# A 3x3 convolution with residual: x loaded as fp32 through the hardware queue of residual and output, and cast to bf16 while it is packed

## The chip, the core and the metric

The kernel runs on one core of a Trainium2 chip. The core has five engines that matter here: TensorE (PE) multiplies matrices, VectorE (DVE) and ScalarE (ACT) work element by element, GpSimd (POOL) and SyncE (SP) here mainly issue transfers. Sixteen DMA engines move data between the chip's memory (HBM) and the core's on-chip memory (SBUF, 128 partitions). A DMA that is issued by SP or ACT goes through a hardware queue; one that is issued by POOL goes through a software queue, and the cast of x during the transfer is written as such a DMA. The metric is the device time of one execution in microseconds, as a median over runs.

## The reference

A batch of 16 images with 64 channels of 64 x 64 pixels is convolved with a 3 x 3 kernel (64 channels in, 64 out, padding 1), and a residual is added. Inputs and output are fp32.

```python
x_pad = np.pad(x, ((0, 0), (0, 0), (pad, pad), (pad, pad)), mode='constant')
for b, co, ci, kh, kw in all_indices:
    output[b, co] += weight[co, ci, kh, kw] * x_pad[b, ci, kh:kh+h, kw:kw+w]
return (output + residual).astype(np.float32)
```

Read from HBM are x and residual, 16.78 MB each, and 0.15 MB of weights; written are 16.78 MB.

## The kernel before

**Tiling.** Two images make a pair: 2 x 64 channels fill the 128 partitions, 4096 pixels each. There are eight pairs. A pair of x is loaded into a tile `xr` (bf16, five buffers, L48), a pair of the residual into a tile `ro` (fp32, one tile for each of the eight pairs, L47). The result is added into `ro` in place and stored from there, so a DMA of a pair moves 2.097 MB on the HBM side.

**Loads.** `load_x` (L53, L54) is issued by POOL and casts fp32 to bf16 during the transfer. `load_ro` (L56, L57) is issued by SP. At the start the weights are loaded by ACT's queue (L102), x pairs 0 to 4 by POOL (L103 to L106) and all eight residual pairs by SP (L107, L108). The x pairs 5 to 7 are issued by POOL as buffers come free: in `pack`, after the second image of a pair has been packed (L67, L68).

**Packing.** `pack(n)` (L59 to L68) puts image n into a tile `xp` (four buffers) so that even rows lie in partitions 64 to 127 and odd rows, shifted by one, in partitions 0 to 63. DVE copies the even rows (L65), ACT the odd rows (L66), 64 x 2048 elements each, bf16 to bf16.

**Convolution.** `convolve(n)` (L70 to L86) does 6 x 4 matmuls of 128 x 128 by up to 512 columns: three horizontal shifts, two row offsets, four chunks of eight rows of pairs. The weights are in a tile `wl` with zero blocks, so that one matmul makes even and odd output rows together. The result fills one of two PSUM buffers.

**Add and store.** `add(n)` (L88 to L98) adds PSUM and residual on DVE with two instructions of 64 x 2048 elements (L94). After the second image of a pair SP stores the pair (L98).

**Weights.** They are loaded into `wdup` (64 x 576 fp32), doubled by DVE (L117), transposed by PE in nine small steps with an identity matrix that POOL makes (L121), and cast into `wl` by six DVE copies (L132).

**Order.** The schedule is written out by hand: each engine runs its instructions in the order in which the program names them. `pack(0)` and `pack(1)` come first; then, for n from 0 to 15, `convolve(n)`, `pack(n + 2)`, `add(n)`. SP's queue has the eight residual loads and behind them the eight stores; POOL's queue has the x loads.

Of the kernel before, what the change touches and what calls it, by code (L numbers as in the profile page):

```python
# [1 line left out]

# [5 lines left out]

FP32 = mybir.dt.float32
BF16 = mybir.dt.bfloat16  # L10
ADD = mybir.AluOpType.add


@with_exitstack
def kernel(
    ctx: ExitStack,
    tc: tile.TileContext,
    x: bass.AP,
    weight: bass.AP,
    residual: bass.AP,  # L20
    out: bass.AP,
):
    nc = tc.nc

    B, C, H, W = x.shape
    CO = weight.shape[0]
    K = weight.shape[2]
    assert C == 64 and CO == 64 and K == 3 and H == 64 and W == 64 and B == 16

    NPIX = H * W  # L30
    NPAIR = B // 2
    J = H // 2
    JC = 8
    NCHUNK = J // JC
    NXR = 5

    res_bc = residual.rearrange("b c h w -> (b c) (h w)")
    out_bc = out.rearrange("b c h w -> (b c) (h w)")
    x_bc = x.rearrange("b c h w -> (b c) (h w)")
    w_flat = weight.rearrange("co ci kh kw -> co (ci kh kw)")  # L40

    pool = ctx.enter_context(tc.tile_pool(name="pool", bufs=1))
    psum = ctx.enter_context(tc.tile_pool(name="psum", bufs=2, space=bass.MemoryType.PSUM))

    wdup = pool.tile([64, 2, 576], FP32)
    ident = pool.tile([64, 64], FP32)
    ro = [pool.tile([128, NPIX], FP32, name=f"ro{p}") for p in range(NPAIR)]  # L47
    xr = [pool.tile([128, NPIX], BF16, name=f"xr{i}") for i in range(NXR)]  # L48

    xp = [pool.tile([128, J + 1, W], BF16, name=f"xp{i}") for i in range(4)]  # L50
    wl = pool.tile([128, 2, 3, 2, 64], BF16)

    def load_x(p):  # L53
        nc.gpsimd.dma_start(out=xr[p % NXR][:, :], in_=x_bc[128 * p : 128 * p + 128, :])  # L54

    def load_ro(p):  # L56
        nc.sync.dma_start(out=ro[p][:, :], in_=res_bc[128 * p : 128 * p + 128, :])  # L57

    def pack(n):  # L59

        p, im = divmod(n, 2)
        hp = slice(64 * im, 64 * im + 64)
        x4 = xr[p % NXR].rearrange("q (j two w) -> q j two w", two=2, w=W)
        t = xp[n % 4]
        nc.vector.tensor_copy(out=t[64:128, 0:J, :], in_=x4[hp, :, 0, :])  # L65
        nc.scalar.copy(out=t[0:64, 1 : J + 1, :], in_=x4[hp, :, 1, :])  # L66
        if im == 1 and p + NXR < NPAIR:  # L67
            load_x(p + NXR)  # L68

    def convolve(n):  # L70
        t = xp[n % 4]
        ps = psum.tile([128, NCHUNK, JC, W], FP32, name="ps")
        order = [(1, 0), (1, 1), (0, 0), (0, 1), (2, 0), (2, 1)]
        for i, (kw, d) in enumerate(order):
            xlo, xhi = max(0, 1 - kw), min(W, W + 1 - kw)
            for c in range(NCHUNK):
                j0 = JC * c
                nc.tensor.matmul(  # L78
                    out=ps[:, c, :, xlo:xhi],
                    lhsT=wl[:, d, kw, :, :].rearrange("q r c -> q (r c)"),  # L80
                    rhs=t[:, j0 + d : j0 + d + JC, xlo + kw - 1 : xhi + kw - 1],
                    start=i == 0,
                    stop=i == len(order) - 1,
                    skip_group_check=True,
                )
        return ps  # L86

    def add(n, ps):  # L88
        p, im = divmod(n, 2)
        hp = slice(64 * im, 64 * im + 64)  # L90
        o4 = ro[p].rearrange("q (j two w) -> q j two w", two=2, w=W)
        psj = ps.rearrange("q c j w -> q (c j) w")
        for par in range(2):
            nc.vector.tensor_tensor(  # L94
                out=o4[hp, :, par, :], in0=psj[64 * par : 64 * par + 64, :, :], in1=o4[hp, :, par, :], op=ADD
            )
        if im == 1:
            nc.sync.dma_start(out=out_bc[128 * p : 128 * p + 128, :], in_=ro[p][:, :])  # L98


    with tc.manual_schedule():
        nc.scalar.dma_start(out=wdup[:, 0, :], in_=w_flat[:, :])  # L102
        load_x(0)  # L103
        make_identity(nc, ident[:, :])
        for p in range(1, NXR):
            load_x(p)  # L106
        for p in range(NPAIR):  # L107
            load_ro(p)  # L108

        for t in xp:  # L110
            nc.vector.memset(t[0:64, 0, :], 0.0)  # L111
            nc.vector.memset(t[64:128, J, :], 0.0)  # L112
        nc.vector.memset(wl[0:64, 0, :, 1, :], 0.0)  # L113
        nc.vector.memset(wl[64:128, 1, :, 0, :], 0.0)  # L114


        nc.vector.tensor_copy(out=wdup[:, 1, :], in_=wdup[:, 0, :])  # L117
        wdup3 = wdup.rearrange("p d (ci t) -> p (d ci) t", t=9)
        tp = psum.tile([128, NCHUNK, JC, W], FP32, name="ps")
        for t in range(9):  # L120
            nc.tensor.transpose(out=tp[:, t // 8, t % 8, :], in_=wdup3[:, :, t], identity=ident[:, :])  # L121
        tpf = tp.rearrange("p c j w -> p (c j) w")
        for half, d, par, kh in (
            (0, 0, 0, 0),
            (1, 0, 0, 1),
            (1, 0, 1, 0),
            (0, 1, 0, 2),
            (0, 1, 1, 1),
            (1, 1, 1, 2),
        ):  # L130
            hp = slice(64 * half, 64 * half + 64)
            nc.vector.tensor_copy(out=wl[hp, d, :, par, :], in_=tpf[hp, 3 * kh : 3 * kh + 3, :])  # L132

        pack(0)
        pack(1)
        for n in range(B):
            ps = convolve(n)
            if n + 2 < B:
                pack(n + 2)
            add(n, ps)  # L140


# [1 line left out]
_INS = ['x', 'weight', 'residual']  # L144
_OUTS = [((16, 64, 64, 64), 'float32')]


# [23 lines left out]
```

## Time and profile before

| what | value |
|---|---|
| median of 7 runs | 125.5 us (125.38 to 125.86) |
| the profiled execution | 125.64 us, of which the span from first to last instruction is 123.9 |
| PE, DVE, ACT, POOL busy | 89.3, 87.6, 31.6, 4.9 us |
| a pack copy on ACT, on DVE | 1.90 us, 0.69 us (64 x 2048, bf16) |
| an add on DVE | 2.29 us (64 x 2048, fp32) |
| matmuls of the convolution | 88.1 us in all, from 18.36 to 106.42 |
| weights, issue to landing | 10.1 us |
| x pair, residual pair, output pair: median from issue to landing | 42.4, 43.5, 31.3 us |
| granted TensorE clock, mean | 0.941 |

The profile shows one execution. Its page has the busy share of each engine in 40 equal slices of the span (a 9 is 90% or more), the share of the 16 DMA engines that were busy and the GB/s that landed, a table of DMA queues, and the chain of work that ended last. A table by windows gives, for a stretch of time, the busy time of PE, weight loads, DVE, ACT and POOL, then the granted clock, the DMA share and the GB/s. A DMA's time from issue to landing includes the time in which it waited behind others in its queue.

### The profile page before, as it was taken

The numbers are of one execution on the slowest core, as the hardware profiler recorded it, in microseconds if no ns is written. First come the engines' busy times: TensorE is split into PE (matmuls) and PEld (weight loads), VectorE is DVE, ScalarE is ACT, GpSimd is POOL, SyncE is SP. The second block draws the span as 40 slices with busy tenths as digits, with TensorE's granted clock in tenths as the row PEclk, the third lists the DMA queues.
The fourth block names the chain that finished last, engine by engine and source line by source line (L and its number), as shares of the span: only waits on it lengthen the run. The fifth ranks groups of instructions, "written<-read, shape, count | busy, mean of one in ns | idle before, by whom it ended". The sixth has DMA issues, their size and how long they took to land.

```text
span 123.9 us, 1002 instructions
## 1 busy us (share of the span) xinstructions
PE 89.3 (72%) x393; PEld 38.4 (31%) x393; DVE 87.6 (71%) x65; ACT 31.6 (26%) x17; POOL 4.9 (4%) x14
## 2 busy tenths in 40 slices
PE   0003109999999999999999999999999999300000
PEld 0003003344344444443434344444444444000000
DVE  3001640059999999999999999999999999780000
ACT  4000065056038009108307505603800000000000
POOL 6400001000100010000000000000000000000000
PEclk9999999999999999999999999999999999965555
DMA  5999999999999999999999999999999999999990
GB/s 111 359 326 302 357 312 296 328 339 299 312 341 299 325 339 307 307 344 331 302 341 336 296 336 320 296 320 421 434 423 418 450 429 434 439 429 429 423 386 16
DMA packets 3540, 42.15 MB, mean 340 GB/s; under 512 B 400, under 2 KB 400, under 8 KB 464
## 3 DMA queue, kind: packets, MB, share of 16 engines
q1 hardware_dynamic: 2304, 33.56, 64.8%
q0 software_dynamic: 1152, 8.39, 32.3%
q10 hardware_dynamic: 80, 0.15, 0.3%
q8 instruction: 3, 0.05, 0.1%
q14 instruction: 1, 0.01, 0.0%
HBM read 33.70 MB, written 16.78 MB: 408 GB/s over the span
## 4 chain that ended last, share of the span: by engine, by line
PE 71%; DMA 12%; DVEq 2%; DVE 2%; ACT 2%; issue 1%; POOLq 0%
PE ps L78 71%; DMA xr<-in_x_dram 12%; DVEq L166 2%; DVE ro L94 2%; ACT xp L66 2%; POOLq L155 0%; POOLq masks.py:199 0%
## 5 line engine op out<-in xcount | busy, mean ns | idle before, releaser
L78 PE MATMUL ps<-xp,wl 128*128 128x504 bf16 (+1 forms) x384 | 88.0, 388 | 5.7 <-ACT xp L66 5.7
L94 DVE TENSOR_TENSOR ro<-ps,ro 64x2048 f32<-64x2048 f32 x32 | 73.2, 2289 | 1.5 <-PE ps L78 0.9
L78 PEld LDWEIGHTS <-wl 128*128 128x128 bf16 x384 | 37.3, 99 | 56.1 <-issue 11.3
L66 ACT COPY xp<-xr 64x2048 bf16<-64x2048 bf16 x16 | 30.4, 1897 | 56.4 <-DMA xr<-in_x_dram 56.2
L65 DVE COPY xp<-xr 64x2048 bf16<-64x2048 bf16 x16 | 11.0, 689 | 10.5 <-DMA xr<-in_x_dram 10.1
L121 PE MATMUL ps<-ident,wdup 64*128 64x64 f32 x9 | 1.3, 319 | 11.4 <-DVE wdup L117 11.4
L117 DVE COPY wdup<-wdup 64x576 f32<-64x576 f32 x1 | 0.5, 452 | 8.7 <-DMA wdup<-in_weight_dram 8.7
L54 POOL DMA_DIRECT2D xr<-in_x_dram x8 | 4.4, 555 | 38.7 <-DVE xp L65 21.9
L121 PEld LDWEIGHTS ps<-ident,wdup 64*128 64x128 f32 x9 | 1.1, 206 | 11.4 <-issue 11.4
L132 DVE CAST wl<-ps 64x192 bf16<-64x192 f32 x6 | 2.0, 352 | 1.5 <-PE ps L121 1.4
L66 ACT ACT_TABLE_LOAD x1 | 1.3, 1283 | 1.3 <-PEq L155 1.3
L111 DVE MEMSET xp<- 64x32 uint32 x4 | 0.3, 85 | 0.9 <-PEq L155 0.8
L112 DVE MEMSET xp<- 64x32 uint32 x4 | 0.3, 85 | 0.2
masks.py:199 POOL TENSOR_SCALAR_AFFINE_SELECT ident<-ident 64x64 f32<-64x64 f32 x1 | 0.2, 228 | 0.1
L114 DVE MEMSET wl<- 64x96 uint32 x1 | 0.1, 138 | 0.1
L113 DVE MEMSET wl<- 64x96 uint32 x1 | 0.1, 138 | 0.1
masks.py:197 POOL MEMSET ident<- 64x64 f32 x1 | 0.2, 171 | 0.0
L155 POOL MEMSET const-float32-0.0<- 128x1 f32 x1 | 0.1, 104 | 0.2 <-issue 0.2
L155 POOL MEMSET const-bfloat16-1.0<- 128x1 bf16 x1 | 0.1, 107 | 0.0
L155 POOL MEMSET const-uint8-127<- 128x1 uint8 x1 | 0.1, 107 | 0.0
L155 POOL MEMSET const-float32-1.0<- 128x1 f32 x1 | 0.1, 103 | 0.0
## 6 DMA issues: line engine op xcount, KB each, us to landing
ro<-in_residual_dram SPq DMA_DIRECT2D x8, 2048.0 KB, 43.5
out_dram<-ro SPq DMA_DIRECT2D x8, 2048.0 KB, 31.3
xr<-in_x_dram POOLq DMA_DIRECT2D x8, 1024.0 KB, 42.4
wdup<-in_weight_dram ACTq DMA_DIRECT2D x1, 144.0 KB, 10.1
```

Source lines behind the costliest of these rows:

```text
L54: nc.gpsimd.dma_start(out=xr[p % NXR][:, :], in_=x_bc[128 * p : 128 * p + 128, :])
L65: nc.vector.tensor_copy(out=t[64:128, 0:J, :], in_=x4[hp, :, 0, :])
L66: nc.scalar.copy(out=t[0:64, 1 : J + 1, :], in_=x4[hp, :, 1, :])
L78: nc.tensor.matmul(out=ps[:, c, :, xlo:xhi], lhsT=wl[:, d, kw, :, :].rearrange("q r c -> q (r c)"), rhs=t[:, j0 + d : j0 + d + JC, xlo + k ...
L94: nc.vector.tensor_tensor(out=o4[hp, :, par, :], in0=psj[64 * par : 64 * par + 64, :, :], in1=o4[hp, :, par, :], op=ADD)
L111: nc.vector.memset(t[0:64, 0, :], 0.0)
L112: nc.vector.memset(t[64:128, J, :], 0.0)
L117: nc.vector.tensor_copy(out=wdup[:, 1, :], in_=wdup[:, 0, :])
L121: nc.tensor.transpose(out=tp[:, t // 8, t % 8, :], in_=wdup3[:, :, t], identity=ident[:, :])
L132: nc.vector.tensor_copy(out=wl[hp, d, :, par, :], in_=tpf[hp, 3 * kh : 3 * kh + 3, :])
L155: nc = _bacc.Bacc("TRN2", target_bir_lowering=False, num_devices=1)
L166: with _tile.TileContext(nc) as tc:
```

## The change

x is loaded as fp32 by SP, in turn with the residual: x0, residual 0, x1, residual 1, x2, residual 2 at the start, and then one further pair of each when n is even and a buffer is to come free. `xr` holds fp32 and has three buffers in place of five. The cast to bf16 is done by the copies of `pack`; both halves are now copied by ACT, except for images 0 and 1, where DVE still copies the even rows. The weights are loaded by POOL, and `wdup` has no tile of its own: it lies in the tile of residual pair 7, whose load comes late. Stores are issued apart from `add`: pairs 0 to 3 after images 9, 11, 13 and 15, which in SP's order is behind all loads, and pairs 4 to 7 at the end.

```diff
-    NXR = 5
+    NXR = 3
...
-    wdup = pool.tile([64, 2, 576], FP32)
...
-    xr = [pool.tile([128, NPIX], BF16, name=f"xr{i}") for i in range(NXR)]
+    xr = [pool.tile([128, NPIX], FP32, name=f"xr{i}") for i in range(NXR)]
...
+    wdup = ro[NPAIR - 1][0:64, 0:1152].rearrange("p (d f) -> p d f", d=2)
...
-        nc.gpsimd.dma_start(out=xr[p % NXR][:, :], in_=x_bc[128 * p : 128 * p + 128, :])
+        nc.sync.dma_start(out=xr[p % NXR][:, :], in_=x_bc[128 * p : 128 * p + 128, :])
...
-        nc.vector.tensor_copy(out=t[64:128, 0:J, :], in_=x4[hp, :, 0, :])
+        first = nc.vector.tensor_copy if n < 2 else nc.scalar.copy
+        first(out=t[64:128, 0:J, :], in_=x4[hp, :, 0, :])
         nc.scalar.copy(out=t[0:64, 1 : J + 1, :], in_=x4[hp, :, 1, :])
-        if im == 1 and p + NXR < NPAIR:
-            load_x(p + NXR)
...
-        if im == 1:
-            nc.sync.dma_start(out=out_bc[128 * p : 128 * p + 128, :], in_=ro[p][:, :])
+
+    def store(p):
+        nc.sync.dma_start(out=out_bc[128 * p : 128 * p + 128, :], in_=ro[p][:, :])
...
-        nc.scalar.dma_start(out=wdup[:, 0, :], in_=w_flat[:, :])
-        load_x(0)
+        nc.gpsimd.dma_start(out=wdup[:, 0, :], in_=w_flat[:, :])
         make_identity(nc, ident[:, :])
-        for p in range(1, NXR):
+        for p in range(NXR):
             load_x(p)
-        for p in range(NPAIR):
             load_ro(p)
...
             if n + 2 < B:
                 pack(n + 2)
+            p, im = divmod(n, 2)
+            if im == 0 and p + NXR < NPAIR:
+                load_x(p + NXR)
+                load_ro(p + NXR)
             add(n, ps)
+            if n >= 9 and n % 2 == 1:
+                store((n - 9) // 2)
+        for p in range((B - 9) // 2 + 1, NPAIR):
+            store(p)
```

## The prediction

> **What bounds the kernel now.** I read the page's slices first, then the table of DMA queues, then the windows by stage, then the chain of work that ended last.
>
> ```profile
> PE   0003109999999999999999999999999999300000
> ...
> DMA  5999999999999999999999999999999999999990
> GB/s 111 359 326 302 357 312 296 328 339 299 312 341 299 325 339 307 307 344 331 302 341 336 296 336 320 296 320 421 434 423 418 450 429 434 439 429 429 423 386 16
> ```
>
> The DMA engines are full from the second slice to the last but one. TensorE starts in the sixth slice and is done four slices before the end. So the transfers set the time, although PE is busy throughout the middle. The GB/s row counts bytes where they land, which is why it rises to about 430 after slice 27: from there only stores are left.
>
> ```profile
> q1 hardware_dynamic: 2304, 33.56, 64.8%
> q0 software_dynamic: 1152, 8.39, 32.3%
> ...
> HBM read 33.70 MB, written 16.78 MB: 408 GB/s over the span
> ```
>
> The columns are packets, MB landed and share of 16 engines' span. The shares sum to 97.5% with the small queues: 120.8 of 123.9 us. The rest, 3.1 us, is the start and the end.
>
> ```profile
> 0.56 0.06 issue
> 0.62 0.02 POOLq L155
> 0.64 0.59 issue
> 1.23 0.00 POOLq masks.py:199
> 1.23 15.16 DMA xr<-in_x_dram
> ...
> 18.36 88.06 PE ps L78 x384
> 106.42 0.02 issue
> 106.45 2.29 DVE ro L94
> 108.73 2.31 DVEq L166
> ```
>
> The chain (start, length, what) goes through PE, but that is misleading: it ends at 111.0, when the last store is issued. That store then waits for the transfers ahead of it and takes 11.5 us to land (the shortest of the eight), more than twice the 4.9 us that 2.097 MB take at 429 GB/s. So compute ends about 6 us before it would delay the last store: 11.5 less 4.9, less about 1 us for starting and finishing.
>
> **The bytes of the change.** HBM traffic does not change: x is read as fp32 in both kernels, 50.48 MB in all. What lands in SBUF grows by 8.39 MB, because x no longer shrinks on the way. Does that cost DMA time? The table of queues answers: q0 took 32.3% of 123.9 = 40.0 us for 16.78 MB read and 8.39 landed; q1 took 64.8% = 80.3 us for 33.56 MB, or 40.1 us per 16.78. A packet of x costs what its source bytes cost, so the cast in the DMA saves nothing and the extra landed bytes cost 0.1 us at most.
>
> [...]
>
> **The rate of the transfers.** What remains is how fast loads run on one queue instead of two in turn.
>
> ```profile
> 2.00:3.50 1.50, 0.00 (x0) 0.00 (x0) 0.14 (x1) 0.59 (x1) 1.43 (x5) 1.00 0.68 175
> 3.50:5.50 2.00, 0.00 (x0) 0.00 (x0) 0.00 (x0) 0.00 (x0) 0.95 (x2) 1.00 0.94 390
> 12.00:82.00 70.00, 64.33 (x282) 27.49 (x281) 58.33 (x40) 26.56 (x14) 1.59 (x3) 1.00 1.02 320
> 86.00:119.00 33.00, 20.41 (x93) 8.65 (x91) 23.94 (x12) 3.35 (x2) 0.00 (x0) 0.85 1.00 429
> ```
>
> The last two columns are DMA share and GB/s landed. In 12 to 82 x and residual share the engines; both are read through at about 85 us, so equally. Of two packets one lands half its bytes, so the source rate is 320 x 4/3 = 427 GB/s. In 86 to 119 one hardware queue works alone (stores) at 429. The trace's packet records say the same with more digits: a 16 KB packet takes 624 ns when the queues alternate, 611 when one queue works alone, loads at the start among them; counted per engine, one such packet goes every 612 ns in the mixed stage and every 608 in the stores. Before 5.5 us only the residual's queue moves bulk data, so the rows at 2.0 and 3.5 are loads on one hardware queue: 0.68 of the engines at first, then 0.94 and 390 GB/s.
>
> The loads are 2 x 16.78 = 33.55 MB. At 427 they take 78.6 us. At 429 they take 78.2, a gain of 0.4; by the packet counts (128 packets per engine, 4.4 ns each) 0.56. I take **0.5 us**. The bounds: at 390 GB/s (the 3.5 to 5.5 row, still warming up) 86.0 us, a loss of 7.4; and at the 451 that the two half-microsecond windows from 4.5 to 5.5 average (463 and 439), 74.4 us, a gain of 4.2. I choose the store row because it is a steady stage of one hardware queue, while the other two are short and belong to the start; the packets of 611 ns among the first loads speak for it.
>
> The start is unchanged: SP issues its first DMA at 0.75 us in both, now x instead of residual. The weights are 0.15 MB in both.
>
> [...]
>
> **The edits that cost nothing, and their cover.** All lie beside full DMA engines.
>
> - Weights go from ACT's queue to POOL's, ahead of the identity. Their landing took 10.1 us with three queues; POOL's issue is at 1.23. From landing to the last cast of wl the trace has 10.89 to 14.76 = 3.9 us. With bounds of 6 and 15 us for the landing, wl is ready between 11 and 20; I take 14.
> - x0 goes first, alone on its queue: the first residual landed 10.8 us after its issue, sharing; x0 should land by 9 to 11.
> - The DVE halves of images 0 and 1 now read fp32: between 0.69 (the bf16 copy) and 2.29 us (the fp32 add of the same shape) each. Convolution 0 then starts near 15 (12 to 23) instead of 18.4.
> - From image 2 on ACT does both halves. The bf16 copy is 1.90 us; for fp32 input I take the same, bounds 0.69 and 2.29. So 3.8 us (at most 4.6) per image, under PE's 88.1/16 = 5.5. DVE loses 0.69 per image and keeps 2 x 2.29 = 4.6.
> - Supply: a pair x, residual takes 2 x 4.9 = 9.8 us, and PE uses a pair in 11.0. So PE does not starve: done at 15 + 88.1 = 103, last add at 108 (105 to 116).
> - SP's order: the load of x(p+3) waits for ACT's last pack of pair p. When x(p) lands, five DMAs (24 us) are still queued; packing takes 4 x 1.9 = 7.6 us, a few more where the tile xp is not yet free. So over 10 us of work is always queued, and residual(p+3), behind the waiting load on SP, is not late. The four early stores are issued only after all loads, with their adds long done; they too find the queue full.
> - The ninth hardware DMA already waits for the first ("SPq L57 <- DMA wdup" 6.3 us). If each DMA waits for the eighth before it, seven are still queued: no hole.
> - The last store's turn comes at 120.4 - 4.9 = 115.5 us. Its add is done near 108: 7 us of cover. Once convolution 0 starts after 23, each us counts in full.
>
> **The sum.** The profiled run took 125.64 us: span 123.9 and 1.7 around it. 125.64 - 0.5 = 125.14. The median of the runs, 125.5, lies 0.14 lower, so in terms of a median I say **125.0**.
>
> **Rivals.**
>
> 1. *Loads alone on one queue leave gaps*, which the software queue's packets fill today. For it: the 0.68 and 0.94 shares before 5.5 us, and the mixed stage's share of 1.02 against 1.00, so packets overlap more with two queues. Against it: stores on one queue run at 429, and the first loads' packets settle at 611 ns. It decides from a load rate below 425 GB/s (78.9 us, 0.25 more than now). Midway between 390 and 427, at 408, loads take 82.2 and the time is 129.1; 420 gives 126.8. Chance 0.18.
> 2. *Nothing changes*: a load packet has its slot of 612 ns whichever queue it is in, because HBM reads set it. The trace cannot part reads from the alternation after 12 us. Time 125.5. Chance 0.20.
> 3. *Compute ends late*: weights behind a full queue start convolution 0 at 25 instead of 15; the last add is then at 118, 2.2 us behind the last store's turn: 127.7. The 7 us of cover speak against it. Chance 0.04.
> 4. *A larger gain*: loads near 440 (76.3 us), or the engines finishing closer together at the end; now the last slices show 386 and 16 GB/s, so some stop before others. Time 123 to 124.2. Chance 0.08.
>
> The forecast itself, 124.2 to 125.25, has 0.50.
>
> **Numbers.** About 0.2% (0.25 us) is what a measurement of this kernel can tell from no change. Faster by more: forecast and rival 4, 0.58. Within: rival 2, 0.20. Slower: rivals 1 and 3, 0.22. The range leaves out most of rival 4 (0.07) and the part of rivals 1 and 3 above 126.8 (0.13): 124.2 to 126.8.
>
> **What would show it.** In the changed profile: one bulk queue with about 97% of the engines' time and 50.3 MB; GB/s near 429 from the third slice on, level over loads and stores; no DMA slice under 9 between; convolution 0 near 15 us and the last add near 108, with several us before the last transfer; a span near 123.4. A load stage of 415 or less, with a share below 1.0, would be rival 1; a DMA slice of 7 or 8 in the middle would mean that SP was late; a last store that starts moving as soon as it is issued, rival 3.

## The result, and the profile after

The changed kernel takes **125.95 us** (median of 25 runs, 125.55 to 126.47) against 125.44 for the kernel before (62 runs, 125.08 to 125.86). The ratio is 1.0038, with a 95% interval from 1.0030 to 1.0046: slower by about 0.5 us, where 0.5 us faster was forecast. The profiled execution took 126.02 us with a span of 124.2.

The page of the changed kernel, its slices (TensorE, DMA share, GB/s landed):

```profile
PE   0004499999999999999999999999999800000000
...
DMA  5999999999999999999999999999999999999990
GB/s 106 383 339 427 427 427 427 422 427 427 422 438 433 433 427 422 427 427 427 427 422 417 433 433 422 433 438 427 427 427 422 427 438 438 427 443 427 433 401 37
```

The DMA engines are as full as before, with no hole in the middle, and GB/s is level over loads and stores. One slice stands out: the third, 339 GB/s, with the engines marked full. The convolution starts one slice earlier (14.2 us against 18.4) and ends earlier.

The table of queues (packets, MB, share of 16 engines):

```profile
q1 hardware_dynamic: 3456, 50.33, 96.2%
q0 software_dynamic: 48, 0.15, 0.4%
q8 instruction: 3, 0.05, 0.2%
```

All bulk data is on one queue. A line of before is missing, "q14 instruction: 1": it will matter.

The end of the chain of waits (start, length, what):

```profile
14.21 84.84 PE ps L78 x384
99.04 0.02 issue
99.06 2.28 DVE ro L94
101.35 2.31 DVEq L173
```

Compute is done at 103.7 us and the last store then takes 19 us to land: compute is further from the bound than before. The copies that moved are no cost in themselves:

```profile
L67 ACT CAST xp<-xr 64x2048 bf16<-64x2048 f32 x14 | 26.5, 1896 | 20.2 <-DMA xr<-in_x_dram 20.0
L68 ACT CAST xp<-xr 64x2048 bf16<-64x2048 f32 x16 | 30.4, 1898 | 8.0 <-DMA xr<-in_x_dram 7.7
...
L67 DVE CAST xp<-xr 64x2048 bf16<-64x2048 f32 x2 | 2.4, 1220 | 0.0
```

An fp32 copy on ACT takes 1.90 us like the bf16 one, and ACT's idle time waits for x.

The windows by stage answer the question of the rate (DMA share and GB/s are the last two columns):

```profile
3.50:5.50 2.00, 0.00 (x0) 0.00 (x0) 0.00 (x0) 0.00 (x0) 0.00 (x0) 1.00 0.95 401
12.00:82.00 70.00, 67.80 (x306) 30.34 (x307) 57.35 (x29) 49.52 (x27) 0.00 (x0) 1.00 1.01 428
86.00:119.00 33.00, 13.03 (x61) 5.68 (x58) 15.83 (x7) 1.15 (x1) 0.00 (x0) 0.76 1.01 431
```

The loads run at 428 GB/s landed; before they landed 320, which is 427 at the source. Counted in packets of 16 KB at the source, 1826 go by in these 70 us, against 1825 before: in both one every 612 ns per engine, when the time of instruction fetches is left out. The loads alone on one queue gained nothing; the gap to the stores (431, every 608 to 609 ns) stayed.

So where do the 0.5 us come from? Two places, at the two ends. First the window from 6 to 12 us, before:

```profile
6.00:12.00 6.00, 0.56 (x5) 0.59 (x6) 0.45 (x1) 0.00 (x0) 0.00 (x0) 1.00 1.05 315
```

and after:

```profile
6.00:12.00 6.00, 1.26 (x9) 1.11 (x9) 1.44 (x4) 2.29 (x2) 0.00 (x0) 1.00 1.01 377
```

The 315 hold x at half its source bytes; the 377 do not. Counted in packets of 16 KB read or stored, 150 went by before and 130 after. In the packet records of the changed kernel bulk packets stretch from 611 to as much as 1026 ns between 5.8 and 8.4 us; the weights' packets alternate with them from 5.7 to 7.7. Before, the weights had alternated (4.9 to 9.3 us) with packets of 624 ns, of which after 5.5 us none took more than 696.

Second, the very end, in SP's own waits (total, times, longest). Before:

```profile
SPq L166 <- PEq L166: 0.6, 2, 0.5
```

After:

```profile
SPq L173 <- PEq L173: 0.9, 2, 0.8
```

These are the two meetings after the last store has landed, where the engines wait for one another. The longer one grew by 0.3 us. The last instructions show who is late. In the trace PE, ACT, DVE and SP each end with a drain, which raises the semaphore that the meeting waits for. VectorE's last drain starts at 123.39 us and takes 19 ns before; after, it starts at 123.90, 0.4 us behind the drains of the other engines, and takes 124 ns.

The two profiled executions add up like this: the last landing is 0.50 us later (122.56 to 123.05); SP then passes through its remaining semaphores in 0.09 us where it had needed 0.51, so 0.42 are won back; the meetings take 1.10 us where they had taken 0.79, 0.31 lost. Together 0.39; the spans differ by 0.37.

### The profile page after: what moved, and what is told of

Same layout as the page of the kernel before. It is cut to its first block, busy times and chain, and to the rows that moved or that the text cites. A ratio compares the mean times of both kernels' runs of the same rounds, so it can differ in the third digit from the quotient of the medians.

```text
span 124.2 us, 994 instructions
## 1 busy us (share of the span) xinstructions
PE 86.1 (69%) x393; PEld 39.0 (31%) x393; DVE 79.0 (64%) x51; ACT 58.2 (47%) x31; POOL 1.3 (1%) x7
## 4 chain that ended last, share of the span: by engine, by line
PE 69%; DMA 6%; DVE 5%; DVEq 2%; issue 1%; POOLq 0%
PE ps L78 68%; DMA ro<-in_weight_dram 6%; DVEq L173 2%; DVE ro L94 2%; DVE wl L131 2%; PE ps L120 1%; DVE xp L67 1%; DVE ro L116 0%; POOLq L162 0%; POOLq masks.py:199 0%
## 5 line engine op out<-in xcount | busy, mean ns | idle before, releaser
L78 PE MATMUL ps<-xp,wl 128*128 128x504 bf16 (+1 forms) x384 | 84.8, 385 | 3.2 <-DVE xp L67 3.2
L78 PEld LDWEIGHTS <-wl 128*128 128x128 bf16 x384 | 37.9, 99 | 49.9 <-DVE xp L67 3.4
L67 ACT CAST xp<-xr 64x2048 bf16<-64x2048 f32 x14 | 26.5, 1896 | 20.2 <-DMA xr<-in_x_dram 20.0
L68 ACT CAST xp<-xr 64x2048 bf16<-64x2048 f32 x16 | 30.4, 1898 | 8.0 <-DMA xr<-in_x_dram 7.7
L120 PE MATMUL ps<-ident,ro 64*128 64x64 f32 x9 | 1.3, 320 | 9.7 <-DVE ro L116 9.7
L116 DVE COPY ro<-ro 64x576 f32<-64x576 f32 x1 | 0.5, 451 | 7.0 <-DMA ro<-in_weight_dram 7.0
L120 PEld LDWEIGHTS ps<-ident,ro 64*128 64x128 f32 x9 | 1.1, 205 | 9.7 <-issue 9.7
L67 DVE CAST xp<-xr 64x2048 bf16<-64x2048 f32 x2 | 2.4, 1220 | 0.0
L103 POOL DMA_DIRECT2D ro<-in_weight_dram x1 | 0.6, 647 | 0.8 <-POOLq L162 0.8
```

Of the source, the lines that this page charges most:

```text
L67: first(out=t[64:128, 0:J, :], in_=x4[hp, :, 0, :])
L78: nc.tensor.matmul(out=ps[:, c, :, xlo:xhi], lhsT=wl[:, d, kw, :, :].rearrange("q r c -> q (r c)"), rhs=t[:, j0 + d : j0 + d + JC, xlo + k ...
L103: nc.gpsimd.dma_start(out=wdup[:, 0, :], in_=w_flat[:, :])
```

## The experiments

Time is the median in us; "ratio" is against the kernel before as measured beside it, with its 95% interval. "By 12 us" counts bulk packets of 16 KB at the source that have gone by 12 us; "mean end" is when the 16 engines had finished the last store, on average, and "last" the slowest of them; "meeting" is the longest wait in the SP line above. The last four come from one profiled execution of each.

| kernel | time | ratio | by 12 us | mean end | last | meeting |
|---|---|---|---|---|---|---|
| before | 125.44 | | 227 | 120.85 | 122.17 | 0.5 |
| changed | 125.95 | 1.0038 (1.0030 to 1.0046) | 209 | 121.53 | 122.72 | 0.8 |
| weights on ACT | 125.97 | 1.0050 (1.0035 to 1.0065) | 216 | 121.30 | 122.70 | 0.8 |
| before, weights on POOL | 125.57 | 1.0017 (1.0004 to 1.0029) | 208 | 121.60 | 122.58 | 0.5 |
| weights twice | 127.14 | 1.0142 (1.0116 to 1.0168) | 185 | 122.44 | 124.13 | 0.8 |
| weights in own tile | 126.02 | 1.0052 (1.0033 to 1.0071) | 212 | 121.43 | 122.95 | 0.8 |
| weights first on SP | 125.83 | 1.0033 (1.0021 to 1.0044) | 219 | 121.01 | 122.35 | 0.8 |
| that, and a load into 64 partitions | 127.14 | 1.0135 (1.0121 to 1.0149) | 197 | 121.99 | 123.47 | 0.8 |
| that, and a load into 128 partitions | 126.26 | 1.0067 (1.0050 to 1.0084) | 211 | 121.35 | 122.76 | 0.8 |
| x on ACT's hardware queue | 125.85 | 1.0033 (1.0021 to 1.0045) | 221 | 121.07 | 122.40 | 0.8 |
| before, weights first on SP | 125.55 | 1.0015 (1.0004 to 1.0025) | 226 | 120.97 | 122.14 | 0.5 |
| cast in the DMA again | 125.97 | 1.0041 (1.0026 to 1.0056) | 209 | 121.56 | 122.61 | 0.8 |
| fp32 through the software queue | 125.87 | 1.0040 (1.0025 to 1.0054) | 214 | 121.32 | 122.56 | 0.8 |
| more instructions on VectorE | 125.72 | 1.0025 (1.0013 to 1.0037) | 209 | 121.61 | 122.96 | 0.5 |
| that, and weights first on SP | 125.55 | 1.0015 (1.0006 to 1.0023) | 218 | 121.11 | 122.39 | 0.4 |

The column "by 12 us" gives "mean end" to within 0.2 us in all rows: a packet less is 611/16 = 38 ns, so the 18 packets between before and changed are 0.69 us, and the mean ends differ by 0.68. From 12 to 82 us all fifteen move between 1823 and 1829 packets, with whatever queue and type x has. So after the start the bulk transfers differ by 0.2 us at most.

### The weights at the start

The first theory was that the weights on the software queue are the loss. Four kernels: the weights back on ACT; the kernel before with the weights on POOL; the weights loaded twice; the weights in a tile of their own.

```diff
-        nc.gpsimd.dma_start(out=wdup[:, 0, :], in_=w_flat[:, :])
+        nc.scalar.dma_start(out=wdup[:, 0, :], in_=w_flat[:, :])
```

> The changed kernel, with the weights issued by ACT's hardware queue as before, nothing else undone. Theory A (the weights' transfer through the software queue slows the bulk packets beside it: in the changed profile 129.8 bulk packets' worth of 16 KB moved between 6 and 12 us, against 150.2 before, a loss of 20 packets x 611 ns / 16 engines = 0.8 us): the window 6 to 12 goes from 377 GB/s to about 405 and the time falls by 0.5 to 0.8, to 125.2 to 125.5, level with the kernel before. Theory B (the loss belongs to x running on the single hardware queue at the start, whatever the weights do): the window stays near 377 and the time near 125.95. Theory C (nothing at the start; the loads on one queue are slower throughout): 125.95 as well, with the window 12 to 82 below that of before.

Measured: 125.97. The window from 6 to 12 us rose only part of the way:

```profile
6.00:12.00 6.00, 1.27 (x9) 1.11 (x9) 0.89 (x3) 2.07 (x2) 0.00 (x0) 1.00 1.01 395
```

Bulk packets beside ACT's weights still took up to 791 ns. The mean end came 0.23 us earlier, the slowest engine did not. Theory A as worded (the software queue) falls; so does C's premise for the rate (428 in the load stage). The window is above B's 377, though the time is as B and C had it.

```diff
-        nc.scalar.dma_start(out=wdup[:, 0, :], in_=w_flat[:, :])
+        nc.gpsimd.dma_start(out=wdup[:, 0, :], in_=w_flat[:, :])
```

> The kernel before, with only the weights moved to POOL's software queue, ahead of x pair 0. Theory A: slower than before by 0.5 to 0.8, to 125.9 to 126.2, with hardware packets of the residual stretched beyond 700 ns while the weights move. Theories B and C: within 0.2 of 125.44.

Measured: 125.57, ratio 1.0017, that is 0.2 us slower (0.05 to 0.36). The stretch is there as theory A said (packets of up to 1036 ns, 208 by 12 us), but the time moved by much less than the 0.5 to 0.8 that it asked for. The mean end is 0.75 us later; the slowest engine only 0.41, and SP's last semaphores take 0.08 us instead of 0.51, because the last store is now among the last that it looks at.

```diff
         nc.gpsimd.dma_start(out=wdup[:, 0, :], in_=w_flat[:, :])
+        nc.gpsimd.dma_start(out=wdup[:, 1, :], in_=w_flat[:, :])
...
-        nc.vector.tensor_copy(out=wdup[:, 1, :], in_=wdup[:, 0, :])
```

> The changed kernel, with the weights loaded twice by POOL (the second load in place of VectorE's copy that doubles them), so twice the suspected cost. Theory A: the slow stretch is about twice as long and the time rises by 0.5 to 1.2 over 125.95, to 126.4 to 127.1, of which 0.4 would be the packets themselves. Theories B and C: at most 0.4 more, the engines' time of 0.15 MB more.

Measured: 127.14, 1.2 us more, just above what A expected. Of these, 0.4 are an estimate of the added packets' own time, from the 0.3% of the engines' span that the weights took before; by 12 us 24 packets fewer than in the changed kernel have gone by. So here the second load cost more than the 0.4 estimated for its own packets.

```diff
-    wdup = ro[NPAIR - 1][0:64, 0:1152].rearrange("p (d f) -> p d f", d=2)
+    wdup = pool.tile([64, 2, 576], FP32)
```

> The changed kernel, with the weights in a tile of their own instead of in residual tile 7, still loaded by POOL. If the place in SBUF matters in theory A, the slow stretch shrinks and the time falls toward 125.4; if the queue matters, it stays at 125.95 within 0.2. Theories B and C: 125.95.

Measured: 126.02, within the 0.2 that was allowed for. The tile's address does not matter to what these runs can tell.

### Taking the alternation away, and its place

```diff
-        nc.gpsimd.dma_start(out=wdup[:, 0, :], in_=w_flat[:, :])
+        nc.sync.dma_start(out=wdup[:, 0, :], in_=w_flat[:, :])
```

> The changed kernel, with the weights issued by SP as the first DMA of its queue, so that on each engine they go ahead of x pair 0 and do not alternate with it. Moving them to ACT changed nothing in the time (125.97), but in that run too the bulk packets beside them took up to 790 ns instead of 611. Theory D (small packets that write partitions 0 to 63 beside full-rate fp32 loads slow the bulk packets of all engines, from whichever queue they come): the window 6 to 12 us goes from 377 to about 428 GB/s, no packet after 4 us exceeds 680 ns, and the time falls by 0.5 to 0.9, to 125.1 to 125.4. Theory C (no loss at the start matters; the end is set by something later): 125.95 within 0.2.

Measured: 125.83, above theory D's band and inside theory C's, though near its lower edge. By the ratios it is 0.06 us below the changed kernel (1.0033 against 1.0038, with overlapping intervals). The stretch is gone:

```profile
6.00:12.00 6.00, 0.53 (x2) 0.36 (x3) 3.89 (x7) 2.45 (x2) 0.00 (x0) 1.00 1.02 437
```

But the weights hold up the first bulk packets, so 219 are through by 12 us, not 227, and something else keeps the kernel 0.4 us behind the one before. The start is at most a small part of the loss in time.

The next two add a load of the same 0.15 MB that nothing reads, on POOL, into 64 partitions or into 128.

```diff
+        nc.gpsimd.dma_start(out=dummy[:, :], in_=w_flat[:, :])
```

> As the run with the weights first on SP, and POOL loads the same weights once more beside x pair 0, into 64 partitions of a tile that nothing reads. Theory D: the slow stretch is back; 0.5 to 1.0 above the run with the weights first on SP. If the loss was not the alternation: no more than 0.3 above it.

```diff
+        nc.gpsimd.dma_start(out=dummy[:, :], in_=w_flat.rearrange("co (h f) -> (co h) f", h=2))
```

> The same, with the additional load spread over all 128 partitions in rows half as long: the same bytes, twice the rows. [...] Rival E (the number of small packets in alternation is the cause): the loss is as large as with 64 partitions or larger, 0.6 to 1.5.

Measured: 127.14 and 126.26, that is 1.31 and 0.43 us above 125.83. Spread over all partitions, the same bytes in twice the rows cost a third. The bulk packets beside the load took up to 851 ns with 64 partitions and no more than 632 after 4 us with 128, so the stretch differed between the two places. Two things keep the times from being its clean price. The packet records show 32 packets of 4608 bytes for either load: only the rows were doubled, so the count of packets (rival E) was not put to the test. And the load into 64 partitions began at 2.7 us and held up the bulk, most of which started from 3.7 on, while the load into 128 began at 4.1, behind the first bulk packets; why they begin so far apart is not known. With 64 partitions the cost is above the 0.5 to 1.0 of theory D; with 128 it is below the 0.6 to 1.5 of rival E. Why the place should matter is not shown.

```diff
-        nc.sync.dma_start(out=xr[p % NXR][:, :], in_=x_bc[128 * p : 128 * p + 128, :])
+        nc.scalar.dma_start(out=xr[p % NXR][:, :], in_=x_bc[128 * p : 128 * p + 128, :])
```

> The changed kernel, with x on ACT's hardware queue and residual and output on SP's: two fp32 queues in alternation, the weights on POOL as in the change. Two questions. First, the rate of the loads from 12 to 82 us: if the reads set it (rival 2 of the prediction), 427 to 428 GB/s as with one queue and as before; if alternation costs what the prediction took, 425 or less. Second, the start: in theory D by place the weights stretch the bulk packets to 900 ns and more as in the change, and the time stays at 125.95 within 0.3; if a third ring beside the weights was what kept the kernel before free of it, packets stay near 624 ns and the time falls to about 125.4.

Measured: 125.85, loads at 427 GB/s with two fp32 queues in alternation, every 612 ns. So the forecast of rival 2 of the prediction holds: the slot of a load was 612 ns before, with one queue of fp32 loads and with two. Its reason (HBM reads set the slot) is not shown, and is doubtful: with the weights first on SP's queue, loads went every 608 ns from 12 to 28 us. At the start packets beside the weights took up to 941 ns, so the third queue did not protect them here. What protected the kernel before is then perhaps that x landed as bf16, half the bytes, beside the weights (315 GB/s landed from 6 to 12 us); in the kernel before with the weights on POOL, where only the fp32 residual ran beside them, packets stretched. That is argued from these four traces and not tried by itself.

```diff
-        nc.scalar.dma_start(out=wdup[:, 0, :], in_=w_flat[:, :])
+        nc.sync.dma_start(out=wdup[:, 0, :], in_=w_flat[:, :])
```

> The kernel before, with only the weights moved, to the front of SP's queue. In before the weights took 0.4 us of the engines' time but stretched no packet, so there is little to win: 125.44 within 0.25, by theory D as by the others. If the weights ahead of the bulk delay its first packets (they started 0.8 us later in the changed kernel with this edit), up to 0.4 slower.

Measured on the kernel before: 125.55, ratio 1.0015, inside the band. Nothing to win there.

### The engines that fetch instructions

In the traces of the full kernels three engines finish last, the slowest 1.0 us and more behind the mean, and there are three fetches of 16 KB of instructions ("q8"). One group of matmuls instead of six takes most of TensorE's program away; such a kernel leaves out five sixths of the convolution. It is tried on the kernel before, on the changed kernel and on the changed kernel with the weights first on SP, called light below.

```diff
-        order = [(1, 0), (1, 1), (0, 0), (0, 1), (2, 0), (2, 1)]
+        order = [(1, 0)]
```

> The kernel before, with one of the six matmul groups of each image instead of six: five sixths of the convolution are left out, all transfers, packs and adds stay. Theory F: the end is set by the few DMA engines that also fetch instructions (16 KB each, three times in the span, 0.88 to 0.95 us here); in the trace of before three engines finish at 121.2, 121.6 and 122.2 us and the other thirteen by 121.1. With far fewer instructions most fetches go and the time falls by 0.7 to 1.2, to 124.2 to 124.7. If the fetches do not matter, it stays at 125.4 within 0.2.

> The changed kernel, with the same five sixths of the convolution left out. In its trace three engines finish at 122.5 to 122.7 us and the other thirteen by 121.9, and a fetch takes 1.04 to 1.08 us. Theory F: the time falls by 0.8 to 1.3, to 124.6 to 125.2. What remains between this and the light kernel before is then the start (theory D: 0.78 us of engine time lost from 6 to 12 us, part of it covered by unequal engines): 0.3 to 0.6. If the longer fetches were all of the change's loss, the two light kernels are equal within 0.1.

> The changed kernel with the weights first on SP's queue, and five sixths of the convolution left out: neither the start's alternation nor most fetches. With both theories it is level with the light kernel before within 0.2, or faster by up to 0.5 if the loads keep the slot of 608 ns that they had until 28 us in the full run. If it stays 0.3 or more above the light kernel before, a third cause is at work.

Measured: 124.50, 124.68 and 124.77 (ratios 0.9926, 0.9946 and 0.9946, each within 0.0014). The queues of the light changed kernel have no "q8" any more:

```profile
q1 hardware_dynamic: 3456, 50.33, 97.2%
q0 software_dynamic: 48, 0.15, 0.4%
```

Theory F holds for both kernels: without the fetches the slowest engine ends 0.4 to 0.6 us behind the mean; before and changed have 1.3 and 1.2. The matmuls are gone too, but in the kernel before the mean end comes only 0.2 us earlier (120.65), which is about what three fetches of 0.9 us make over 16 engines; the gain of 0.9 us in time is in the slowest engine. That the late engines are the ones that fetched is inferred: the packet records do not name the engine. Of the difference between the kernels 0.2 to 0.3 remains, with and without the alternation (the third light kernel was expected within 0.2), so the fetches are not its cause or not all of it, and the alternation alone is not either.

### The load, or the rest of the change

Two kernels put x back on POOL's software queue: one with the cast, which has both parts of this edit, and one in fp32, which has the second part alone. Two more are their light forms.

```diff
-    xr = [pool.tile([128, NPIX], FP32, name=f"xr{i}") for i in range(NXR)]
+    xr = [pool.tile([128, NPIX], BF16, name=f"xr{i}") for i in range(NXR)]
...
-        nc.sync.dma_start(out=xr[p % NXR][:, :], in_=x_bc[128 * p : 128 * p + 128, :])
+        nc.gpsimd.dma_start(out=xr[p % NXR][:, :], in_=x_bc[128 * p : 128 * p + 128, :])
```

> The changed kernel with only its load of x undone: x goes through POOL's software queue and is cast in the DMA; order, packs on ACT, three buffers and late stores stay. Weights are on the same queue, ahead of x. If the change's loss comes from how x is loaded (theory G: fp32 on the hardware queue): level with the kernel before that has its weights on POOL, 125.4 to 125.7, and a fetch of instructions takes 0.88 to 0.98 us. If it comes from the order or the packs: 125.85 to 126.0, and a fetch takes 1.03 to 1.11 us.

> The changed kernel with x as fp32, but through POOL's software queue: twice the landed bytes, two kinds of queue. If the landed fp32 bytes matter (theory G1): as the change, 125.8 to 126.1, fetches of 1.03 to 1.11 us. If the hardware queue matters (theory G2): as before, 125.4 to 125.6, fetches of 0.88 to 0.98 us.

> As the run that casts in the DMA, with five sixths of the convolution left out, so that the fetches go. Theory G with the fetches as its larger part: 124.5 to 124.7, within 0.15 of the light changed kernel (124.68). If the way of loading costs something besides start and fetches, the difference between the light kernels is 0.2 or more.

> x as fp32 through the software queue, with five sixths of the convolution left out. Fetches as the larger part: 124.5 to 124.8, as the other light kernels, whatever the full kernel with this load gave.

Measured: 125.97 and 125.87, light 124.98 and 124.70. **Theory G falls:** with the cast back in the DMA the kernel is as slow as the change. A fetch took 0.93 to 0.95 us there and 1.04 to 1.10 with fp32, so the fetches were longer with fp32, but the time did not follow. (The light kernel with the cast is even 0.3 above the light changed one, outside what was expected; that is not explained.) The loss must be in what these kernels share with the change. In the one with the cast:

```profile
SPq L173 <- PEq L173: 0.9, 2, 0.8
```

That wait is 0.8 us in each kernel so far whose VectorE has lost the 14 copies of the packs (65 instructions in the trace), and 0.5 in each of those that have them (85). The latter also fetch 8 KB of instructions on "q14" near 80 us; in the others that fetch comes after the end.

### VectorE's program

```diff
+    spare = pool.tile([64, 64], BF16)
...
     def add(n, ps):
...
+        for _ in range(2):
+            nc.vector.memset(spare[:, :], 0.0)
         for par in range(2):
```

> The changed kernel, with two small memsets of a spare tile on VectorE before each add (32 in all, 85 ns each, in VectorE's idle time). Theory H: in every kernel here whose VectorE runs the shorter program of the change (65 instructions against 85) VectorE's last drain starts 0.2 to 0.5 us late and takes 124 to 143 ns instead of 19, and the 8 KB fetch of instructions that lies near 80 us before comes after the end; the other engines wait for it. With the longer program the drain is early and takes 19 ns again, the fetch lies inside the run, and the time falls by 0.25 to 0.4, to 125.55 to 125.7. If the drain is late for another reason, or the late drain costs nothing: 125.95 within 0.15.

> The same memsets, and the weights first on SP's queue, so that neither the late drain nor the alternation at the start is left. If the two are the change's whole loss: 125.4 to 125.6, level with the kernel before within 0.15. If it stays at 125.7 or more, a further cause is at work.

Measured: 125.72, a little above the expected band and outside the other theory's; and 125.55, as expected. The changed kernel with 32 more instructions on VectorE, the waits of SP:

```profile
SPq L176 <- PEq L176: 0.6, 2, 0.5
```

and its queues:

```profile
q8 instruction: 3, 0.05, 0.2%
q14 instruction: 1, 0.01, 0.0%
```

The fetch is inside the run again (66.5 us), the drain takes 19 ns again and starts with the others', and the two meetings take 0.80 us again instead of 1.10. The kernel is faster by adding work: 0.23 us by the medians, 0.16 by the ratios (1.0038 to 1.0025, whose intervals overlap). For the pair with the weights first on SP it is 0.28 by the medians (125.83 to 125.55) and 0.23 by the ratios (1.0033 to 1.0015). Theory H holds for the length of the program and the meeting; the gain in time is at or below the lower edge of what it forecast. That the drain waits for that fetch itself is not shown: in the changed trace the fetch starts at 124.5 us, behind the drain.

With both edits the kernel is at 1.0015 (1.0006 to 1.0023), about 0.2 us behind the kernel before; the two together took 0.3 of the 0.5 us away, clear of the intervals. Its start is still 9 packets behind (0.34 us of engine time), and SP's last semaphores take 0.25 us against 0.51. No version that does the whole convolution beats the kernel before.

The table allows one more comparison, with the weights in the same place and the longer program on VectorE in both kernels. With the weights first on SP, the kernel before and the changed one with more on VectorE both have a ratio of 1.0015. With the weights on POOL they have 1.0017 and 1.0025, with overlapping intervals. So as far as these runs can tell (about 0.2 us) the load of x as fp32, the order and the packs on ACT, but for what they take from VectorE's program, neither gain nor cost anything. The place of the weights (about 0.2) and the shorter program (0.16 to 0.28) make up the change's 0.5 us, or all but 0.1 of it.

## Why the prediction was wrong

- **The bound** was right: DMA engines full, compute ends early and costs nothing. Convolution 0 started at 14.2 (15 was said), the last add ended at 103.7 (108), ACT's fp32 copy took 1.90 us, and no hole appeared in the queue.
- **The bytes** were right: twice the landed bytes of x cost nothing in the load stage. From 12 to 82 us 428 GB/s landed where 320 had, with 1826 packets of 16 KB at the source against 1825.
- **"I choose the store row"** is the step of the sum that failed. The loads on one queue kept their slot of 612 ns; they did not take the 608 of the stores. Rival 2 forecast this, though not with a reason that is shown, and the run with two fp32 queues confirms it. Where 0.5 us were to be gained nothing was: 1826 packets in the load stage against 1825.
- **"The edits that cost nothing, and their cover"** is the step that turned the sign. The weights were priced by their landing time, as a matter of compute, which has cover; what they do to the bulk packets beside them has none, since the DMA engines are the bound. By 12 us that cost 18 packets, 0.69 us of mean engine time, of which about 0.2 us reaches the time. And the copies taken off VectorE were priced by their 0.69 us each; taking them away cost 0.3 us at the end, in a meeting of engines that the prediction took as fixed, inside the span of 123.9 us and with no term of its own.
- **The rivals** had the sign (slower) only through gaps in the loads and late compute; neither happened. Part of the loss is hidden by SP's shorter check of semaphores, 0.42 us, for which the prediction had no term. The measured 125.95 lies inside the stated range of 124.2 to 126.8, but in the part that was there for the gaps of rival 1: that is luck.

How much of the start's 0.69 us reaches the time is not settled to better than 0.1 to 0.2 us. Putting the weights on POOL in the kernel before cost 0.2 us; moving them to the front of SP's queue gained 0.06 in the changed kernel and 0.13 to 0.17 in the one with more on VectorE. The slowest engine counts, and it need not be the one that met the stretch: with the weights on ACT the mean end came earlier (121.30 against 121.53 us) and the slowest engine did not (122.70 against 122.72).

## What to carry to other kernels

Where the DMA engines are full, price a small transfer by what it does to the large ones beside it (here it stretched them from 611 to as much as 1026 ns), not by its own bytes alone; the partitions it lands in and the moment it starts are worth a run each. When a rate differs between two stages by less than 1%, ask what else differs between them (loads, stores) before giving the gain to an edit. In a kernel that must be right to 0.3%, read the last two microseconds instruction by instruction: what the engines do after the last landing (0.3 us longer in the meetings, 0.4 shorter at the semaphores) was worth as much as the change.

## What the runs showed of the hardware

- A load of 0.15 MB into 64 partitions at the start of full-rate fp32 loads cost 1.31 us, into 128 partitions 0.43; the first began 1.4 us earlier, ahead of the bulk. The engines' own time for it is estimated at 0.4, from the 0.3% of their span that the weights took before.
- Without five sixths of the matmuls, and with them the three fetches of 16 KB of instructions, both kernels are 0.9 to 1.3 us faster. The slowest DMA engine then ends 0.4 to 0.6 us behind the mean instead of 1.2 to 1.3.
- With a shorter program on VectorE (65 instructions against 85) the closing meetings took 0.3 us longer; 32 idle memsets took that away.
- With the weights ahead of the bulk on one queue, loads of the changed kernel went every 608 ns until about 28 us and every 612 from then on. What changes at that point stays open.
